# Sliding-window attention on one core: two key blocks folded into one score tile, parted again on GpSimd

## The chip, the core and the metric

The kernel runs on one core of one Trainium2 chip. A core has TensorE (PE, matrix products into PSUM), VectorE (DVE), ScalarE (ACT), GpSimd (POOL, no access to PSUM) and SyncE (SP, which issues the transfers here). Each engine works through its own list of instructions in a fixed order and waits on semaphores for the others. The metric is the device time of one execution in microseconds.

## The reference

Two decoder layers over 1024 tokens of width 1024. Each layer has a token-mixing part, of which one half is attention with eight query heads of 64, two key/value heads and a learned sink per head; the other half is a pooling mixer; then an output projection and a SwiGLU feed-forward. The attention is what the change touches:

```python
diff = qi + BLOCK - kj                      # qi: query in its block of 128, kj: key in two blocks of 128
valid = (diff >= 0) & (diff < WINDOW) & (key_abs >= 0)          # WINDOW = 128
scores = jnp.where(valid, q @ k_cat * HEAD_DIM ** -0.5, NEG_INF)
probs = softmax(concatenate([scores, sink], -1))[..., :-1]
out = probs @ v_cat
```

A query of index i in its block sees, of its own block, the keys 0 to i, and, of the block before, the keys i+1 to 127. So of the 256 keys of the two blocks exactly 128 are seen, one for every key index: own block's where the index is at most i, the other block's where it is larger. In block 0 there is no block before.

## The kernel before, in words

All products are made in split precision: an operand is copied to a rounded high part (`hi`, on ScalarE) and a low part (`lo = x - hi`, on VectorE), by the helper `split` (L220, L221), and a product is three matmuls, hi x hi, hi x lo, lo x hi (`mm3`, L263, L266, L267). Tokens go in two halves of 512 (four blocks of 128 each).

`attention` is a generator that is advanced in step with the dense products (`run` in the layer loop), so that its small matmuls stand among the large ones. Half 0 runs beside the projections of the pooling input and of half 1's queries and keys; half 1 starts beside the output projection of half 0 and goes on beside the projections and the first feed-forward products that follow. It works through groups: a group is one block and one key/value head, four query heads. For a group it

- splits and transposes the queries (`att_queries`, L842 to L851), and at a new block rotates (`att_rotary`, L795 to L800, through a tile `rt`) and transposes the keys of both heads (`att_keys`); the values lie padded with zeros in `vz`, filled by GpSimd casts (L808);
- makes the scores of two heads at a time (`att_scores`): per head two matmuls of 256 columns, both blocks side by side (L866, L867), and one VectorE instruction that adds the mask, scales and takes the row maximum (L869);
- a group later, takes the softmax (`att_softmax`): the sink enters the maximum and the sum by small VectorE steps (L881 to L890) and an exponential (L885); four exponentials of 256 columns on ScalarE (L888), three scalings on VectorE (L894) and one on ScalarE (L896);
- transposes the probabilities of two heads, four tiles of 128x128 (`att_probs`, L904), and splits them into `pth` and `ph` (512 columns: two blocks, two heads);
- multiplies by the values (`att_values`): per block and pair of heads three matmuls of 256 columns, all into one bank `pv`.

In block 0 only the own block's half of all this is done.

What sets the order is the framework's scheduler: it takes the instructions in program order as their priority, plays the program through by its own table of costs, and writes one fixed list for each engine; extra orders within an engine are set by `after`. A tile's tag has a fixed number of buffers (`SMALL`, `SHARED`, `REGIONS`), and a new tile waits until the last use of the one whose buffer it takes.

## Time and profile before

| what | value |
|---|---|
| median of three runs | 1906.67 us (1903.42, 1906.67, 1907.11) |
| span of the profiled execution | 1904.4 us |
| TensorE, VectorE, ScalarE, GpSimd busy | 1864.7, 1540.4, 948.4, 20.0 us |
| mean granted TensorE clock | 0.994 |
| attention, layer 0 | about 66 to 296 us |
| attention, layer 1 | about 1000 to 1236 us |

The page gives the span of one profiled execution (1904.4 us), and no other time of that execution; it lies within the three runs, 2.3 us under their median. Rows of groups read: line, engine, operation, output <- inputs, shapes, count | busy time, mean ns of one | idle time before them and what ended it. Rows of the timeline read: start, duration, engine, line, operation, and in brackets idle time before it. Matmuls are pipelined, so that the durations of neighbours overlap; on the other engines, too, an instruction's listed end lies a little behind the next one's start.

### The profile page before, as it was taken

The numbers are of one execution on the slowest core, as the hardware profiler recorded it, in microseconds if no ns is written. First come the engines' busy times: TensorE is split into PE (matmuls) and PEld (weight loads), VectorE is DVE, ScalarE is ACT, GpSimd is POOL, SyncE is SP. The second block draws the span as 40 slices with busy tenths as digits, with TensorE's granted clock in tenths as the row PEclk, the third lists the DMA queues.
The fourth block names the chain that finished last, engine by engine and source line by source line (L and its number), as shares of the span: only waits on it lengthen the run. The fifth ranks groups of instructions, "written<-read, shape, count | busy, mean of one in ns | idle before, by whom it ended". The sixth has DMA issues, their size and how long they took to land.

```text
span 1904.4 us, 26019 instructions
## 1 busy us (share of the span) xinstructions
PE 1864.7 (98%) x8954; PEld 1540.3 (81%) x8954; DVE 1540.4 (81%) x2889; ACT 948.4 (50%) x1791; POOL 20.0 (1%) x67
## 2 busy tenths in 40 slices
PE   7999999999999999999999999999999999999998
PEld 5887788888888788888888868888887888888886
DVE  7899886668898888788879988846888888867687
ACT  4875795654222223445558667845622222234452
POOL 0000000000000000000000000000000000000000
PEclk9999999999999999999999989999999999999999
DMA  9345563655555665944554464536654565574343
GB/s 341 112 144 161 161 221 125 191 172 193 194 183 188 205 210 172 320 143 150 172 179 139 126 181 164 178 111 209 214 189 146 198 216 197 199 249 157 117 141 114
DMA packets 229540, 341.86 MB, mean 180 GB/s; under 512 B 17016, under 2 KB 126472, under 8 KB 229408
## 3 DMA queue, kind: packets, MB, share of 16 engines
q1 hardware_dynamic: 228800, 338.10, 53.8%
q10 hardware_dynamic: 576, 2.10, 0.3%
q8 instruction: 70, 1.15, 0.3%
q14 instruction: 62, 0.51, 0.1%
q0 software_dynamic: 32, 0.00, 0.0%
HBM read 267.25 MB, written 72.89 MB: 179 GB/s over the span
## 4 chain that ended last, share of the span: by engine, by line
PE 80%; DVE 10%; DMA 5%; ACT 3%; issue 2%; SPq 0%; DVEq 0%; ACTq 0%; POOL 0%; POOLq 0%
PE acc L263 25%; PE acc L266 24%; PE acc L267 24%; DMA ar<-in_ada_w_dram 2%; DVE lo L221 1%; DVE ada L298 1%; DMA raw<-in_w_up_dram 1%; PE msc L904 1%; PE msc L561 1%; ACT hi L220 1%; PE pv L263 1%; PE pv L266 1%; PE pv L267 1%; ACT raw L554 1%; DVE fn L1162 1%
## 5 line engine op out<-in xcount | busy, mean ns | idle before, releaser
L220 ACT ACTIVATE hi<-raw 128x1024 fp32r<-128x1024 f32 (+1 forms) x388 | 331.8, 868 | 360.1 <-PE acc L266 197.1
L221 DVE TENSOR_TENSOR lo<-raw,hi 128x1024 fp32r<-128x1024 f32 (+1 forms) x388 | 380.2, 987 | 121.3 <-ACT hi L220 116.4
L263 PE MATMUL acc<-t,hi 128*128 128x512 f32 x704 | 274.6, 390 | 2.7 <-ACT hi L220 2.6
L266 PE MATMUL acc<-t,hi 128*128 128x512 f32 x704 | 274.0, 389 | 0.0
L267 PE MATMUL acc<-t,lo 128*128 128x512 f32 x704 | 271.8, 389 | 0.0
L263 PE MATMUL acc<-bh,hi 128*128 128x512 f32 x520 | 202.8, 390 | 0.0
L267 PE MATMUL acc<-bh,lo 128*128 128x512 f32 x520 | 202.4, 389 | 0.0
L263 PE MATMUL acc<-hT,hi 128*128 128x512 f32 x480 | 190.2, 396 | 0.6 <-DVE fn L691 0.6
L266 PE MATMUL acc<-hT,hi 128*128 128x512 f32 x480 | 188.4, 392 | 0.0
L267 PE MATMUL acc<-hT,lo 128*128 128x512 f32 x480 | 187.6, 392 | 0.0
L1162 DVE TENSOR_TENSOR fn<-acc,fn 128x512 f32<-128x512 f32 x220 | 150.3, 685 | 38.2 <-PE acc L267 37.6
L263 PEld LDWEIGHTS acc<-t,hi 128*128 128x128 f32 x704 | 132.2, 188 | 32.1 <-ACT hi L220 5.1
L267 PEld LDWEIGHTS acc<-t,lo 128*128 128x128 f32 x704 | 132.2, 188 | 28.7 <-DVE lo L221 1.2
L266 PEld LDWEIGHTS acc<-t,hi 128*128 128x128 f32 x704 | 132.2, 188 | 27.1
L266 PE MATMUL acc<-ph,hi 128*128 128x512 f32 x320 | 124.7, 390 | 0.0
L1098 ACT ACTIVATE fn<-fn 128x512 f32<-128x512 f32 x44 | 27.9, 633 | 181.7 <-DVE fn L1162 181.7
L263 PEld LDWEIGHTS acc<-bh,hi 128*128 128x128 f32 x520 | 97.6, 188 | 20.2
L267 PEld LDWEIGHTS acc<-bh,lo 128*128 128x128 f32 x520 | 97.6, 188 | 20.2
L298 DVE SCALAR_TENSOR_TENSOR ada<-ar,c_act,ada 128x512 f32<-128x512 f32 x140 | 104.6, 747 | 10.1 <-DMA ar<-in_ada_w_dram 9.7
L263 PE MATMUL acc<-hi 128*128 128x512 f32 x256 | 103.5, 410 | 2.4 <-DVE fn L691 2.0
L263 PEld LDWEIGHTS acc<-hT,hi 128*128 128x128 f32 x480 | 90.2, 188 | 19.2 <-DVE fn L691 1.4
L267 PEld LDWEIGHTS acc<-hT,lo 128*128 128x128 f32 x480 | 90.1, 188 | 18.6 <-issue 0.2
(323 smaller groups left out, 3814.5 us busy)
## 6 DMA issues: line engine op xcount, KB each, us to landing
ar<-in_ada_w_dram SPq DMA_DIRECT2D x160, 256.0 KB
raw<-in_w_gate_dram SPq DMA_DIRECT2D x44, 512.0 KB
raw<-in_w_up_dram SPq DMA_DIRECT2D x44, 512.0 KB
raw<-in_w_in_dram SPq DMA_DIRECT2D x80, 256.0 KB
raw<-keeps SPq DMA_DIRECT2D x40, 512.0 KB
keeps<-fn SPq DMA_DIRECT2D x66, 256.0 KB
two_b<-in_w_down_dram SPq DMA_DIRECT2D x30, 512.0 KB
raw<-keepa SPq DMA_DIRECT2D x25, 512.0 KB
```

The lines of the kernel that those rows point to most:

```text
L220: a = nc.scalar.activation(hi, src, AF.Copy)
L221: v = nc.vector.tensor_sub(lo, src, hi.bitcast(F32))
L263: ins = nc.tensor.matmul(dst, lh, rh, start=first, stop=False)
L266: nc.tensor.matmul(dst, lh, rl, start=False, stop=False)
L267: return nc.tensor.matmul(dst, ll, rh, start=False, stop=last)
L298: ins = nc.vector.scalar_tensor_tensor(acc, w, c_act[:, i : i + 1], acc, op0=ALU.mult, op1=ALU.add)
L554: nc.scalar.activation(hf, bank, AF.Identity, bias=shift, scale=scale)
L561: ins = nc.tensor.transpose(bank[:, t * P : (t + 1) * P], src[t], ident)
L904: nc.tensor.transpose(bank[:, i * P : (i + 1) * P], s[:, ii, ck * P : (ck + 1) * P], ident)
L1098: nc.scalar.activation(g, g, AF.Silu)
L1162: nc.vector.tensor_add(halves_of(dst)[m], bank, halves_of(src)[m])
```

## The change

For a group the scores of both blocks are still made, 256 columns a head. Then they are folded into one tile `S` of 128 columns a head: ScalarE copies the scores of the block before out of PSUM (L865 of the changed kernel; in block 0 a GpSimd fill with -1e30 instead), and VectorE copies the own block's scores over them where the 0/1 mask `own` is set (L869, a predicated copy). The sink stands in column 128 of each head, put there by a GpSimd copy and divided by the scale beforehand, so the maximum (L873, one instruction for four heads), the exponentials (L881, 129 columns) and the sums take it along. One VectorE instruction scales the 4x128 probabilities (L885). They are transposed as four tiles of 128x128 (L893) and split once, both parts in `pth`. GpSimd parts them: L906 writes the own block's part (zero elsewhere) of the high and the low half into two new tiles, L911 then zeroes that part in place, which leaves the block before. In block 0 only the own part is kept, in place (L899). The value products are six matmuls of 512 columns, the own block first.

The small tiles change too: `rt` goes, and the rotation uses the unused end of the `S` tile; `pth` has four buffers for two, `st` nine for twelve; the 128x256 mask becomes a 128x128 one.

```diff
-    SMALL = dict(junk=1, st=12, rs=8, ...)
+    SMALL = dict(junk=1, st=9, rs=8, ...)
-        mix=dict(..., vz=5, rt=1, qT=1, pth=2, pwh=1, pwl=1),
+        mix=dict(..., vz=5, qT=1, pth=4, pwh=1, pwl=1),
...
+    own = const.tile([P, P], F32, name="own")
+    nc.gpsimd.memset(own, 1.0)
     nc.gpsimd.affine_select(
+        out=own, in_=own, pattern=[[-1, P]], compare_op=ALU.is_ge,
+        fill=0.0, base=0, channel_multiplier=1,
     )
...
-    def att_scores(blk, n, u, qT, mx, s):
+    def att_scores(blk, u, qT, kT, S):
...
-        for ii in range(2):
-            nc.vector.tensor_tensor_reduce(
-                out=s[:, ii, cs], in0=bank[:, ii * 2 * P : (ii + 1) * 2 * P][:, cs],
-                in1=mask[:, cs], scale=SCALE, scalar=-3.0e38, op0=ALU.add, op1=ALU.max,
-                accum_out=mx[:, 2 * u + ii : 2 * u + ii + 1],
-            )
+        both = bank.rearrange("p (i o k) -> p i o k", i=2, o=2)
+        dst = S[:, 2 * u : 2 * u + 2, 0:P]
+        if blk:
+            nc.scalar.activation(dst, both[:, :, 0, :], AF.Copy)
+        else:
+            nc.gpsimd.memset(dst, NEG)
+        seen = own.bitcast(I32).rearrange("p (o k) -> p o k", o=1).to_broadcast([P, 2, P])
+        nc.vector.copy_predicated(dst, seen, both[:, :, 1, :])
+
+    def att_max(S):
+        mx = t_("st", [P, 8])[:, :GRP]
+        nc.vector.tensor_reduce(mx, S, axis=mybir.AxisListType.X, op=ALU.max)
+        nc.vector.tensor_scalar(mx, mx, -SCALE, None, op0=ALU.mult)
+        return mx
+
+    def att_softmax(S, nm):
+        sm = t_("st", [P, 8])[:, :GRP]
+        es = t_("st", [P, 8])[:, :GRP]
+        for i in range(GRP):
+            nc.scalar.activation(
+                S[:, i, :], S[:, i, :], AF.Exp, bias=nm[:, i : i + 1], scale=SCALE, accum_out=sm[:, i : i + 1]
             )
...
+        nc.vector.reciprocal(es, sm)
+        nc.vector.tensor_mul(
+            S[:, :, 0:P], S[:, :, 0:P], es.rearrange("p (i o) -> p i o", o=1).to_broadcast([P, GRP, P])
         )
...
+        for i in range(GRP):
+            nc.tensor.transpose(bank[:, i * P : (i + 1) * P], S[:, i, 0:P], ident)
+        seen = [t_("pth", [P, 512], F32R) for _ in range(2)]
+        split(*seen, bank)
+        views = [r.rearrange("p (i q) -> p i q", i=GRP) for r in seen]
...
+        here = [t_("pth", [P, 512], F32R) for _ in range(2)]
+        for v, r in zip(views, here):
+            nc.gpsimd.affine_select(
+                out=r.rearrange("p (i q) -> p i q", i=GRP), in_=v, pattern=[[0, GRP], [1, P]],
+                compare_op=ALU.is_ge, fill=0.0, base=0, channel_multiplier=-1,
+            )
+        for v in views:
+            nc.gpsimd.affine_select(
+                out=v, in_=v, pattern=[[0, GRP], [-1, P]], compare_op=ALU.is_gt,
+                fill=0.0, base=0, channel_multiplier=1,
+            )
+        return [seen, here]
...
-        for ck in range(first, 2):
+        for ck in (1, 0) if blk else (1,):
...
             ins = mm3(
-                pv[:, u * 2 * P : (u + 1) * 2 * P],
-                vh[:, vs].rearrange("p a d -> p (a d)"), vl[:, vs].rearrange("p a d -> p (a d)"),
-                ph[:, cs], pl[:, cs], opening, closing, None if opening else attn["open"],
+                pv, vh[:, vs].rearrange("p a d -> p (a d)"), vl[:, vs].rearrange("p a d -> p (a d)"),
+                *probs[ck], opening, closing, None if opening else attn["open"],
             )
...
-    def attention(h, qkvs, nsink, cat):
+    def attention(h, qkvs, sink, cat):
...
+                both = t_("sb", [P, D])
+                S = both[:, : GRP * (P + 1)].rearrange("p (i k) -> p i k", i=GRP)
+                room = both[:, GRP * (P + 1) :]
...
+                nc.gpsimd.tensor_copy(S[:, :, P : P + 1], sink[:, hs].rearrange("p (i o) -> p i o", o=1))
                 yield
+            flush()
             if prev:
-                att_softmax(pblk, pn, sts, mx, nsink)
+                att_softmax(prev[3], prev[4])
                 yield
...
-                flush()
-                if prev:
-                    late.append((pblk, pn, u, att_probs(pblk, sts[u]), cat, pt))
+                if prev and u == 0:
+                    late.append((prev[0], prev[1], att_probs(prev[0], prev[3]), cat, prev[2]))
```

Since the scheduler places every instruction anew, the order shows what the diff does not. TensorE, layer 0, half 1, the last but one group, before: the transposes of the second pair of heads (L904) stand between the first value products of the first pair.

```order
L904 MATMUL msc<-ident,sb 128x128 x2
L263 MATMUL pv<-pth,vz 128x256
L904 MATMUL msc<-ident,sb 128x128 x2
L263 MATMUL acc<-hT,hi 128x512
L266 MATMUL acc<-hT,hi 128x512
L267 MATMUL acc<-hT,lo 128x512
L266 MATMUL pv<-ph,vz 128x256
L267 MATMUL pv<-pth,vz 128x256
L263 MATMUL pv<-pth,vz 128x256
```

Here three dense matmuls lie between the products with the high part and those with the low part. The same group on TensorE in the changed kernel (lines are five to eleven lower; L893 are the transposes, L860 and L861 the next group's scores, L258, L261 and L262 the three matmuls of `mm3`):

```order
L893 MATMUL msc<-ident,sb 128x128 x4
L860 MATMUL msc<-sa,qT 128x256
L861 MATMUL msc<-sa,qT 128x256
L860 MATMUL msc<-sa,qT 128x256
L861 MATMUL msc<-sa,qT 128x256
L261 MATMUL acc<-hT,hi 128x512
L262 MATMUL acc<-hT,lo 128x512
L258 MATMUL acc<-hT,hi 128x512
L261 MATMUL acc<-hT,hi 128x512
L262 MATMUL acc<-hT,lo 128x512
L258 MATMUL pv<-pth,vz 128x512
L258 MATMUL acc<-hT,hi 128x512
```

All four transposes come together, then four score matmuls and five dense ones, then the first value product; three dense matmuls separate it from the other five, which follow each other. GpSimd at about the same place, before:

```order
L808 CAST vz<-vz_zero 128x64 x6
L784 COPY uT<-halo 128x16
L808 CAST vz<-vz_zero 128x64 x4
L784 COPY uT<-halo 128x16 x3
L808 CAST vz<-vz_zero 128x64 x5
```

and in the changed kernel:

```order
L965 COPY sb<-sk 128x4
L906 AFFINE_SELECT pth<-pth 128x512 x2
L911 AFFINE_SELECT pth<-pth 128x512 x2
L803 CAST vz<-vz_zero 128x64 x2
L965 COPY sb<-sk 128x4
L906 AFFINE_SELECT pth<-pth 128x512 x2
L911 AFFINE_SELECT pth<-pth 128x512 x2
```

Between the casts that it had, GpSimd now has four selections for each group, the own block's high and low part first, and the sink's copy for a group to come ahead of them.

More of the change, by code (lines that the diff above doesn't have):

```diff
@@ L96, in hybrid_decoder_kernel @@
     dr = ctx.enter_context(tc.tile_pool(name="dr", bufs=1, space=DRAM))
-    SMALL = dict(junk=1, st=12, rs=8, ss=4, halo=8, rows=1, cols=2, colp=4, sk=2)
+    SMALL = dict(junk=1, st=9, rs=8, ss=4, halo=8, rows=1, cols=2, colp=4, sk=2)
     SHARED = dict(hT=8, fn=4, raw=2, hi=3, lo=3, sa=2, sb=2, ar=2, ada=1, ph=3, G=1)
     REGIONS = dict(
-        mix=dict(cfa=2, cfb=2, qkv=5, bqkv=1, uT=4, pt=2, vz=5, rt=1, qT=1, pth=2, pwh=1, pwl=1),
+        mix=dict(cfa=2, cfb=2, qkv=5, bqkv=1, uT=4, pt=2, vz=5, qT=1, pth=4, pwh=1, pwl=1),
         up=dict(t2=8, t1=8, t3=8, b22=8, t4=8),
@@ L157, in hybrid_decoder_kernel @@
     ones = ones_r.bitcast(F32)
-    pick_row = t_("rt", [P, 7])
+    pick_row = t_("pth", [P, 7])
     nc.vector.memset(pick_row, 0.0)
@@ new lines, in att_scores @@
+            nc.tensor.matmul(dst, q, kT[1][:, cs], start=False, stop=True)
+        both = bank.rearrange("p (i o k) -> p i o k", i=2, o=2)
[11 more added lines that the diff above has]
+        return mx
@@ L898, in att_probs @@
-    def att_probs(blk, s):
-        bank = msc_bank()
-        for ck in range(0 if blk else 1, 2):
-            for ii in range(2):
-                i = 2 * ck + ii
-                nc.tensor.transpose(
-                    bank[:, i * P : (i + 1) * P], s[:, ii, ck * P : (ck + 1) * P], ident
-                )
-        ph = t_("pth", [P, 512], F32R)
-        pl = t_("ph", [P, 512], F32R)
-        cs = slice(0 if blk else 2 * P, 4 * P)
-        split(ph[:, cs], pl[:, cs], bank[:, cs])
-        return ph, pl
@@ L913, in att_values @@
-    def att_values(blk, n, u, probs, cat, t):
-        if n == 0 and u == 0:
+            nc.tensor.transpose(bank[:, i * P : (i + 1) * P], S[:, i, 0:P], ident)
+        seen = [t_("pth", [P, 512], F32R) for _ in range(2)]
+        split(*seen, bank)
+        views = [r.rearrange("p (i q) -> p i q", i=GRP) for r in seen]
+        if not blk:
+            for v in views:
+                nc.gpsimd.affine_select(
+                    out=v, in_=v, pattern=[[0, GRP], [1, P]], compare_op=ALU.is_ge,
+                    fill=0.0, base=0, channel_multiplier=-1,
+                )
+            return [None, seen]
@@ L1477, in hybrid_decoder_kernel @@
         qkvs[1] = [t_("qkv", [P, QKV]) for _ in range(NT)]
-        att = attention(0, qkvs[0], par["nsink"], cats[0][0])
+        att = attention(0, qkvs[0], par["sink"], cats[0][0])
         def dense():
@@ L1494, in hybrid_decoder_kernel @@
         fn, ss, out0 = mix_out(l, cats[0], G)
-        att = attention(1, qkvs[1], par["nsink"], cats[1][0])
+        att = attention(1, qkvs[1], par["sink"], cats[1][0])
         run(out0, 2 * KD, (side, 4 * ADA), (att, 16))
```

70 lines of the change are left out of this document (23 added, 47 removed).

## The prediction

> **What bounds the kernel now.** I read the page's busy shares first, then a table of stretches around the attention, then single groups and stretches of the timeline.
>
> ```profile
> PE 1864.7 (98%) x8954; PEld 1540.3 (81%) x8954; DVE 1540.4 (81%) x2889; ACT 948.4 (50%) x1791; POOL 20.0 (1%) x67
> core 0: us, PE busy (x) PEld busy (x) DVE busy (x) ACT busy (x) POOL busy (x), PEclk, DMA share, GB/s
> 66.00:158.00 92.00, 90.36 (x572) 77.88 (x571) 85.86 (x259) 72.12 (x181) 3.33 (x11) 1.00 0.43 130
> 158.00:200.00 42.00, 37.38 (x172) 28.30 (x171) 38.23 (x99) 25.54 (x60) 0.00 (x0) 0.92 0.60 176
> 200.00:296.00 96.00, 94.37 (x529) 78.78 (x529) 81.32 (x226) 80.29 (x191) 2.99 (x9) 1.00 0.58 191
> 296.00:940.00 644.00, 642.39 (x2862) 530.08 (x2861) 520.25 (x726) 262.26 (x394) 0.00 (x0) 1.00 0.57 190
> 1098.00:1140.00 42.00, 38.09 (x167) 29.15 (x168) 38.81 (x100) 26.95 (x65) 0.70 (x1) 0.88 0.64 185
> 1140.00:1236.00 96.00, 94.45 (x529) 79.09 (x528) 76.93 (x212) 77.38 (x181) 2.73 (x8) 1.00 0.52 174
> ```
>
> TensorE carries the kernel: 98% busy, and 642.39 of 644 us in the long feed-forward stretch, which the change does not touch. The attention lies in 66 to 296 us and, for layer 1, up to 1236 us. There TensorE is still busy 98% of the time, but VectorE is at 85.86 of 92 us and ScalarE at 80.29 of 96: three engines are near their limit together, and GpSimd is idle. In 158 to 200 and 1098 to 1140 the granted clock falls to 0.92 and 0.88.
>
> Busy TensorE time cannot be used as a price, since matmuls overlap. The price is the step from one start to the next:
>
> ```profile
> L904 PE MATMUL msc<-ident,sb 128*128 128x128 f32 x240 | 41.1, 276 | 2.6 <-DVE sb L894 2.1 <-ACT raw L554 0.6
> L263 PE MATMUL pv<-pth,vz 128*128 128x256 f32 x120 | 35.9, 299 | 1.9 <-ACT pth L220 1.8
> 109.14 0.40 PE L263 MATMUL acc<-hi,hT 128*128 128x512 f32 x1
> 109.37 0.40 PE L266 MATMUL acc<-lo,hT 128*128 128x512 f32 x1
> 143.89 0.28 PE L263 MATMUL pv<-pth,vz 128*128 128x256 f32 x1
> 144.01 0.28 PE L266 MATMUL pv<-ph,vz 128*128 128x256 f32 x1
> 144.61 0.60 PE L904 MATMUL msc<-ident,sb 128*128 128x128 f32 x4
> 144.97 0.36 PE L263 MATMUL acc<-hi,hT 128*128 128x256 f32 x1
> ```
>
> A 512-column matmul steps 0.23 us (109.14 to 109.37), a 256-column one 0.12 us, and four transposes of a 128x128 tile 0.36 us (144.61 to 144.97), so 0.09 us each, although each is listed with some 0.28 us.
>
> **The change, part by part.** A group is four heads of one 128-query block. There are 32 in two layers: 28 in blocks that see a block before them, 4 in block 0.
>
> TensorE. Transposes fall from 240 to 128: 112 x 0.09 = 10.1 us less. The value products become half as many, twice as wide: twelve of 256 columns (12 x 0.12 = 1.44 us) against six of 512 (6 x 0.23 = 1.38 us), and in block 0 six against three; with 30 times that it is some 2.2 us by the finer steps (0.120 and 0.227). Scores stay. Sum: **-12.3 us**. By the mean durations it would be 112 x 0.276 + 180 x 0.2 = 67 us, which is the trap in this profile.
>
> VectorE and ScalarE, also by steps:
>
> ```profile
> L869 DVE CUSTOM_DVE_ANT_0 sb<-msc,mask 128x256 f32<-128x256 f32 x112 | 44.2, 416 | 7.8 <-PE msc L867 7.4
> L888 ACT ACTIVATE sb<-sb,st 128x256 f32<-128x256 f32 x112 | 55.6, 502 | 5.9 <-DVE st L881 5.9
> L888 ACT ACTIVATE sb<-sb,st 128x128 f32<-128x128 f32 x16 | 6.2, 390 | 0.0
> 139.93 0.17 DVE L890 RECIPROCAL st<-st 128x4 f32<-128x4 f32 x1
> 140.01 0.39 DVE L869 CUSTOM_DVE_ANT_0 sb<-msc,mask 128x256 f32<-128x256 f32 x1
> 140.33 0.87 DVE L894 TENSOR_SCALAR sb<-sb,st 128x256 f32<-128x256 f32 x3
> 141.12 0.69 DVE L1002 TENSOR_TENSOR pt<-pt 128x521 f32<-128x521 f32 x1
> 141.74 0.68 DVE L763 TENSOR_TENSOR qkv<-acc,bqkv 128x512 f32<-128x512 f32 x1
> 142.35 0.69 DVE L221 TENSOR_TENSOR ph<-msc,pth 128x512 fp32r<-128x512 f32 x1
> 246.10 0.40 ACT L842 ACTIVATE hi<-qkv 128x256 fp32r<-128x256 f32 x1
> 246.89 0.51 ACT L896 ACTIVATE sb<-sb,st 128x256 f32<-128x256 f32 x1 [0.38 <-DVE st L890]
> ```
>
> VectorE loses per group four masked maxima (4 x 0.32, 140.01 to 140.33), one of two splits (0.61, 141.74 to 142.35), three scalings (0.79, 140.33 to 141.12) and two small steps (2 x 0.08): 2.84 us. It gains two predicated copies, one maximum over 4x129 and one scaling of 4x128. None stands in the trace. A predicated copy has the size and source of the masked maximum, so 0.32 us; above, 0.61 us if it went at the step of a 512-column operation. The other two read 512 columns like the rows of 0.61. That is 1.86 us, or 2.44 us at the upper end: **0.4 to 1.0 us less a group**, 11 to 28 us less in 28 groups. ScalarE loses 0.11 us on each exponential (502 against 390 ns), the sink's own exponential, the scaling (about 0.4 us, like L842's 0.40) and one split (0.60 us, at 141.72 below), and gains two copies of 256 columns (0.40 each at most): some 0.7 us less a group, about 20 us in all. Both engines have slack against TensorE over a whole stage, and the score-to-transpose chain gets a copy, a separate maximum and a negation (0.40 + 0.61 + 0.08) while losing as much (0.44 in exponentials, 0.4 in the scaling, the sink's small steps). I take **0** for the path, with -4 us as the other end, for the stage at 200 us where ScalarE is fullest.
>
> GpSimd takes over the masking: four selections of 128x512 a group, two in block 0, so 120, plus 32 sink copies and 8 fills.
>
> ```profile
> masks.py:199 POOL TENSOR_SCALAR_AFFINE_SELECT G<-G 128x128 f32<-128x128 f32 x1 | 0.3, 299 | 0.1
> L166 POOL TENSOR_SCALAR_AFFINE_SELECT mask<-mask 128x256 f32<-128x256 f32 x1 | 0.4, 391 | 0.0
> 2.97 0.41 POOL L808 CAST vz<-vz_zero 128x64 fp32r<-128x64 f32 x2
> 955.25 2.24 POOL L808 CAST vz<-vz_zero 128x64 fp32r<-128x64 f32 x4 [680.14 <-ACT hT L220]
> 955.24 0.69 DVE L221 TENSOR_TENSOR hT<-ada,hT 128x512 fp32r<-128x512 f32 x1 [1.51 <-ACT hT L220]
> 955.85 1.37 DVE L221 TENSOR_TENSOR lo<-raw,hi 128x512 fp32r<-128x512 f32 x2
> 141.19 0.49 PE L904 MATMUL msc<-ident,sb 128*128 128x128 f32 x3
> 141.72 0.60 ACT L220 ACTIVATE pth<-msc 128x512 fp32r<-128x512 f32 x1 [1.03 <-PE msc L904]
> ```
>
> A selection of 128 columns takes 299 ns, of 256 columns 391 ns: 0.72 ns a column, so **0.58 us** for 512. But GpSimd is slower beside a busy VectorE: two casts alone take 0.41 us, four beside three VectorE operations with two SBUF inputs take 2.24 us, so three of them waited about (2.24 - 4 x 0.2) / 3 = 0.48 us each. A selection then costs 0.58 us alone and about **1.06 us** when its turn falls behind such an operation.
>
> The other way round, VectorE's two splits took 1.37 us for an expected 0.61 + 0.69 = 1.30: about 0.04 us lost to each 64-column cast. A selection has eight times the columns: by that 0.3 us, at the lower end 0.04, at the upper the whole 0.58. With six in ten of VectorE's operations in these stages reading two SBUF tensors (an estimate from the splits from raw, the ada sums and the pool sums among the groups), 120 x 0.3 x 0.6 = 22 us go back to VectorE, about what the folding saved. VectorE as a whole stands where it was. The Trainium skill ("SBUF — State Buffer", "Who interferes with whom") says that a VectorE operation with two SBUF inputs and a GpSimd operation that reads SBUF lock each other out for the whole instruction; the casts agree for GpSimd, and no run here has yet shown the whole instruction for VectorE.
>
> **Where a new wait falls.** The four selections stand between the split and the value products, which are queued on TensorE in a fixed order with dense matmuls behind them. From the last transpose's start (141.19 plus two steps, 141.4) ScalarE's split ends 0.9 us later (142.32) and VectorE's 1.6 us later (142.35 + 0.69). Selection 1 needs the first, 2 the second; 3 and 4 follow in the queue. The fifth product needs selection 4. Without contention that is 1.6 + 3 x 0.58 = 3.3 us after the transposes; with each of three selections behind a VectorE operation, 1.6 + 3 x 1.06 = 4.8 us. In the order shown ahead of this prediction, for the last but one group of a half, TensorE does 4 x 0.12 + 5 x 0.23 before the first product and seven 512-column steps more before the fifth: 3.2 us. So TensorE waits 0.1 to 1.6 us there; I take 0.8. The last two groups of each half are like that: eight groups, 6.4 us. About eight others have 2.7 to 3.5 us of matmuls ahead of the first product; at the contended end they wait 4.8 - 4.0 = 0.8, at the other nothing: 0.25, 2 us. The rest have 6 us or more and do not wait. What TensorE waited for the old split (1.9 us on L263 pv) goes. **+6.5 us**, between -2 (no new wait) and 8 x 1.6 + 8 x 0.8 - 1.9 = +17.
>
> **Sum.** 1904.4 - 12.3 + 0 + 6.5 = 1898.6 against the profiled span. The span is 2.3 us under the median of the runs shown, so I forecast **1901 us**, 0.3% faster.
>
> **Rivals.**
> (1) *The dense stages do not let TensorE's saving through.* VectorE at 93% in 66 to 158 us, and the low clock with the ada sums in 158 to 200, set those stages. Against it: TensorE is at 98% in the same stage. The second halves of the two layers hold 16 of the 28 groups, some six of them in the slow stretches; if only the other ten pass the saving on, it is 10/28 x 12.3 = 4.4 us, the waits take 4 back, and the time is 1906: no change.
> (2) *GpSimd and VectorE block each other.* If every selection holds VectorE for its whole 0.58 us, 120 x 0.58 x 0.6 = 42 us go onto VectorE against 11 to 28 saved; in stages with 93% busy I count half of the 14 to 31 us excess on the path, 11 us, and the products wait at their contended end, 17 us: 1904.4 - 12.3 + 11 + 17 + 2.3 = **1922**; with half of each added cost, 1908, still no change. It decides from the point at which a selection takes over about 0.9 us in its stage. For it: the four casts. Against it: the 0.04 us.
> (3) *The waits vanish.* The planner put other matmuls between the products; -12.3 - 2 - 4 gives 1888.
>
> **How the numbers follow.** Forecast and its near neighbours (1893 to 1903) 0.44, rival 3 0.09, rival 1 0.21, rival 2 0.26. No change means within 0.2% (3.8 us), about what runs of this kernel can tell. The forecast and rival 3 are faster, 0.52 without the forecast's upper edge of 0.01; rival 1 and that edge make 0.22; slower is 0.26. The range leaves one in ten on either side: from 1886, under rival 3, to 1916, more than halfway to the end of rival 2. The likeliest case's own range is 1893 to 1903.
>
> **What would show it.** Right: selections of 0.6 to 1.1 us in the listing; 128 transposes at a step of 0.09; TensorE's idle time before the value products released by POOL, 5 to 10 us over both layers; VectorE's busy time lower by at most 30 us. Wrong: selections of over 1.2 us or VectorE rows of the splits longer than 0.75 us on the mean (rival 2); stages at 66 and 1000 us not shorter (rival 1); no wait released by POOL at all (rival 3). A predicated copy of over 0.7 us would also break the sum.

## The result: slightly slower, where slightly faster was forecast

| | before | changed |
|---|---|---|
| median of 20 runs each | 1907.76 us (1903.42 to 1911.28) | 1911.7 us (1909.27 to 1918.39) |
| ratio to before, 95% interval | 1 | 1.0024 (1.0017 to 1.0031) |
| span of the profiled execution | 1904.4 us | 1911.0 us |

Forecast were 1901 us and 0.3% faster, with 26 in 100 for slower. The profiled execution of the kernel before was a quick one: a run's time lies 1.7 to 2.2 us above its span in the runs here, so its span of 1904.4 us answers to some 1906 us, while the medians of its runs beside the changed kernel and the experiments were 1907.8 to 1909.7 us. So every kernel is compared by its ratio to the runs of the kernel before on the same chip, and traces only stretch by stretch.

The page of the changed kernel gives the busy times, and a table of stretches around the attention the same by stage (columns as before the change):

```profile
PE 1853.3 (97%) x8662; PEld 1516.5 (79%) x8662; DVE 1533.0 (80%) x2569; ACT 923.5 (48%) x1755; POOL 125.7 (7%) x226
```

```profile
66.00:158.00 92.00, 87.87 (x497) 71.23 (x495) 85.27 (x189) 65.61 (x173) 26.57 (x46) 1.00 0.42 130
158.00:200.00 42.00, 37.34 (x176) 29.39 (x177) 37.30 (x82) 25.61 (x68) 4.82 (x9) 0.92 0.61 175
200.00:296.00 96.00, 90.50 (x448) 72.43 (x447) 77.85 (x159) 71.63 (x174) 26.72 (x42) 0.98 0.56 183
1000.00:1098.00 98.00, 93.47 (x540) 77.02 (x538) 90.44 (x196) 67.74 (x177) 28.94 (x52) 1.00 0.44 132
```

TensorE has 292 matmuls less and is busy 11.4 us less, and yet the span is longer: TensorE now stands idle where it worked. ScalarE is 25 us lighter (948.4 to 923.5; forecast: about 20). VectorE, which lost four masked maxima, three scalings and a split per group, is only 7.4 us lighter, and in the stretch at 66 us it still works 85.27 of 92 us (before: 85.86).

The groups of the changed kernel that the steps of the prediction spoke of:

```profile
L893 PE MATMUL msc<-ident,sb 128*128 128x128 f32 x128 | 19.5, 275 | 3.1 <-DVE sb L885 1.5 <-DVE pt L1019 0.8 <-ACT hi L215 0.7
L258 PE MATMUL pv<-pth,vz 128*128 128x512 f32 x60 | 26.1, 436 | 1.5 <-POOL pth L911 1.4
L261 PE MATMUL pv<-pth,vz 128*128 128x512 f32 x60 | 25.7, 428 | 4.1 <-POOL pth L911 3.3 <-POOL pth L906 0.5
L911 POOL TENSOR_SCALAR_AFFINE_SELECT pth<-pth 128x512 fp32r<-128x512 f32 x56 | 46.1, 846 | 0.0
L906 POOL TENSOR_SCALAR_AFFINE_SELECT pth<-pth 128x512 fp32r<-128x512 f32 x56 | 41.0, 732 | 49.6 <-ACT pth L215 45.0 <-DVE pth L216 3.3
L899 POOL TENSOR_SCALAR_AFFINE_SELECT pth<-pth 128x512 fp32r<-128x512 f32 x8 | 6.7, 858 | 4.4 <-DVE pth L216 4.4
L869 DVE COPY_PREDICATED sb<-own,msc 128x256 f32<-128x256 int32 x64 | 28.4, 444 | 6.3 <-ACT sb L865 6.0 <-issue 0.2
L873 DVE TENSOR_REDUCE st<-sb 128x4 f32<-128x516 f32 x32 | 21.8, 681 | 0.2
L885 DVE TENSOR_TENSOR sb<-sb,st 128x512 f32<-128x512 f32 x32 | 21.9, 685 | 0.3
```

The prices that the prediction had to bound came out close to it: a selection 0.73 to 0.86 us on the mean, a predicated copy like the masked maximum it replaces (444 ns, from 416), the reduction and the scaling like any 512-column operation. TensorE's idle time before the value products that GpSimd released is 1.4 + 3.3 + 0.5 = 5.2 us. The forecast had 8.4 us of it (6.4 + 2), and took off the 1.9 us of the old wait to get 6.5; by the rows the net is 5.2 - 1.9 = 3.3 us.

**Which stretch lost it.** The dense matmuls (into `acc`) are the same 7368 in every kernel here. Counting them off and comparing when the same one starts gives what each stretch of the program gained or lost against the profiled execution of the kernel before. The stretches are named by their times there; "rest" is all outside the attention, some 3 to 7 us in almost every kernel, of which the quick profiled execution of the kernel before explains some 2 to 4.

| us against before | 66-165 | 165-210 | 210-310 | 990-1110 | 1110-1150 | 1150-1250 | attention | rest |
|---|---|---|---|---|---|---|---|---|
| changed kernel | +2.2 | -4.0 | +3.6 | +2.5 | -3.7 | +1.3 | +1.9 | +4.7 |
| no selections | -3.4 | -3.9 | -1.1 | +0.4 | -3.7 | -2.6 | -14.3 | +4.4 |
| selections unread | +0.6 | -2.3 | +0.5 | +1.8 | -3.3 | +0.3 | -2.4 | +5.2 |
| no selections, 25 us of VectorE work added | +0.0 | -1.1 | +0.7 | +2.5 | -4.3 | +1.1 | -1.1 | +6.8 |
| no selections, transposes back | -0.5 | -3.9 | +3.0 | -1.1 | -3.4 | +4.5 | -1.4 | +12.5 |
| difference of the values | -2.6 | -4.0 | -0.1 | +0.2 | -5.8 | -0.2 | -12.5 | +3.6 |

The changed kernel is slower in the four stretches where selections run beside the dense products, and quicker in the two between the halves. The gain between the halves does not come from the saved transposes, since it is there with the transposes back as well (-3.9 and -3.4). The other rows are experiments, told next.

### The profile page after: what moved, and what is told of

Same layout as the page of the kernel before. It is cut to its first block, busy times and chain, and to the rows that moved or that the text cites. A ratio compares the mean times of both kernels' runs of the same rounds, so it can differ in the third digit from the quotient of the medians.

```text
span 1911.0 us, 25332 instructions
## 1 busy us (share of the span) xinstructions
PE 1853.3 (97%) x8662; PEld 1516.5 (79%) x8662; DVE 1533.0 (80%) x2569; ACT 923.5 (48%) x1755; POOL 125.7 (7%) x226
## 4 chain that ended last, share of the span: by engine, by line
PE 72%; DVE 14%; DMA 5%; ACT 3%; issue 2%; POOL 1%; SPq 1%; POOLq 0%; DVEq 0%; ACTq 0%
PE acc L258 23%; PE acc L261 23%; PE acc L262 22%; DVE lo L216 2%; DMA raw<-in_w_up_dram 2%; DVE ada L293 2%; DMA ar<-in_ada_w_dram 2%; PE msc L556 1%; ACT hi L215 1%; DVE fn L1169 1%; DMA raw<-in_w_in_dram 1%; POOL pth L911 1%; DVE pth L216 1%; PE pv L261 0%; ACT sb L881 0%
## 5 line engine op out<-in xcount | busy, mean ns | idle before, releaser
L215 ACT ACTIVATE hi<-raw 128x1024 fp32r<-128x1024 f32 (+1 forms) x388 | 332.1, 868 | 371.5 <-PE acc L261 194.4
L216 DVE TENSOR_TENSOR lo<-raw,hi 128x1024 fp32r<-128x1024 f32 (+1 forms) x388 | 383.0, 994 | 123.4 <-ACT hi L215 120.2
L258 PE MATMUL acc<-t,hi 128*128 128x512 f32 x704 | 274.6, 390 | 4.8 <-ACT hi L215 4.8
L261 PE MATMUL acc<-t,hi 128*128 128x512 f32 x704 | 274.0, 389 | 0.0
L262 PE MATMUL acc<-t,lo 128*128 128x512 f32 x704 | 272.0, 390 | 0.0
L258 PE MATMUL acc<-bh,hi 128*128 128x512 f32 x520 | 202.8, 390 | 0.0
L262 PE MATMUL acc<-bh,lo 128*128 128x512 f32 x520 | 202.4, 389 | 0.0
L258 PE MATMUL acc<-hT,hi 128*128 128x512 f32 x480 | 190.5, 397 | 1.2 <-DVE fn L686 1.2
L261 PE MATMUL acc<-hT,hi 128*128 128x512 f32 x480 | 188.5, 393 | 0.0
L262 PE MATMUL acc<-hT,lo 128*128 128x512 f32 x480 | 188.2, 392 | 0.0
L258 PEld LDWEIGHTS acc<-t,hi 128*128 128x128 f32 x704 | 132.1, 188 | 34.2 <-ACT hi L215 7.2
L262 PEld LDWEIGHTS acc<-t,lo 128*128 128x128 f32 x704 | 132.1, 188 | 29.3 <-DVE lo L216 1.9
L261 PEld LDWEIGHTS acc<-t,hi 128*128 128x128 f32 x704 | 132.1, 188 | 27.2
L261 PE MATMUL acc<-ph,hi 128*128 128x512 f32 x320 | 124.7, 390 | 0.0
L293 DVE SCALAR_TENSOR_TENSOR ada<-ar,c_act,ada 128x512 f32<-128x512 f32 x140 | 108.7, 777 | 6.7 <-DMA ar<-in_ada_w_dram 5.7
L262 PEld LDWEIGHTS acc<-bh,lo 128*128 128x128 f32 x520 | 97.6, 188 | 20.5
L258 PEld LDWEIGHTS acc<-bh,hi 128*128 128x128 f32 x520 | 97.6, 188 | 20.1
L258 PEld LDWEIGHTS acc<-hT,hi 128*128 128x128 f32 x480 | 90.6, 189 | 20.2 <-DVE fn L686 2.5
L262 PEld LDWEIGHTS acc<-hT,lo 128*128 128x128 f32 x480 | 90.5, 189 | 18.6
L261 PEld LDWEIGHTS acc<-hT,hi 128*128 128x128 f32 x480 | 90.7, 189 | 17.3
```

Of the source, the lines that this page charges most:

```text
L215: a = nc.scalar.activation(hi, src, AF.Copy)
L216: v = nc.vector.tensor_sub(lo, src, hi.bitcast(F32))
L258: ins = nc.tensor.matmul(dst, lh, rh, start=first, stop=False)
L261: nc.tensor.matmul(dst, lh, rl, start=False, stop=False)
L262: return nc.tensor.matmul(dst, ll, rh, start=False, stop=last)
L293: ins = nc.vector.scalar_tensor_tensor(acc, w, c_act[:, i : i + 1], acc, op0=ALU.mult, op1=ALU.add)
```

## The experiments

Each time is a median, and each ratio is to runs of the kernel before on the same chip.

**Without selections.** First the whole price of GpSimd's part: `att_probs` returns the unparted probabilities, which are then multiplied by both blocks' values (the masking of the values is left out).

```diff
         split(*seen, bank)
-        views = [r.rearrange("p (i q) -> p i q", i=GRP) for r in seen]
-        if not blk:
...
-        here = [t_("pth", [P, 512], F32R) for _ in range(2)]
-        for v, r in zip(views, here):
-            nc.gpsimd.affine_select(
...
-        return [seen, here]
+        return [seen, seen]
```

> The changed kernel without any of the 120 selections: the value products read the unparted probabilities for both blocks, so the masking of the values is left out. Theory 'selections' (waiting or blocking): all that GpSimd costs goes, 9 to 13 us less, 1899 to 1903 us, and TensorE's saving of 12 us shows in full against the kernel before. Theory 'tail': the chain of the last group loses its 2 x 2.2 us of selections but keeps the table loads, 1906 to 1909 us. If the dense stages do not let TensorE's saving through (rival 1 of the prediction): 1905 to 1908 us.

Measured: 1896.24 us, ratio 0.9934 (0.9916 to 0.9951), 12.6 us faster than before. The page of this kernel:

```profile
PE 1846.8 (97%) x8662; PEld 1515.0 (80%) x8662; DVE 1511.5 (80%) x2569; ACT 925.6 (49%) x1755; POOL 32.1 (2%) x106
```

Selections and all that hangs on them cost 0.90% of 1909 us, 17 us. VectorE has the same 2569 instructions as in the changed kernel and is busy 1511.5 us instead of 1533.0: the selections lengthen it by 21.5 us. With GpSimd out of the way the folding comes through. What of it is TensorE's and what VectorE's, this run does not tell.

**Selections that nobody reads.** They have two prices: products that wait for them, and VectorE held up beside them. Here all 120 run, but into tiles that no product reads (masking again left out).

```diff
-        for v in views:
+        for v, r in zip(views, here):
             nc.gpsimd.affine_select(
-                out=v, in_=v, pattern=[[0, GRP], [-1, P]], compare_op=ALU.is_gt,
+                out=r.rearrange("p (i q) -> p i q", i=GRP), in_=v, pattern=[[0, GRP], [-1, P]], compare_op=ALU.is_gt,
...
-        return [seen, here]
+        return [seen, seen]
```

> The changed kernel with as many selections on GpSimd, written to two tiles that no product reads: the value products read the unparted probabilities, so the masking of the values is left out, but GpSimd works as before beside VectorE. If the cost of the selections is that the products wait for them: as without selections, within 2 us (1899 to 1904 us). If it is that GpSimd and VectorE block each other: close to the changed kernel, 1908 to 1912 us.

Measured: 1909.26 us, ratio 0.9997 (0.9987 to 1.0007). So of the 17 us, 0.63% or 12 us stay although nothing waits for a selection; what is left for the waiting is the other 0.27%, 5 us. By stretches of the traces it is 11.9 and 4.3. The page, and the value products, which now wait for GpSimd nowhere:

```profile
PE 1851.3 (97%) x8662; PEld 1516.2 (79%) x8662; DVE 1531.5 (80%) x2569; ACT 926.5 (49%) x1755; POOL 127.6 (7%) x226
```

```profile
L258 PE MATMUL pv<-pth,vz 128*128 128x512 f32 x60 | 25.2, 420 | 1.8 <-ACT pth L215 1.7
L261 PE MATMUL pv<-pth,vz 128*128 128x512 f32 x60 | 24.0, 399 | 0.0
```

The unread copies take as many `pth` buffers as the changed kernel's, but a lack of buffers is not what costs: of the 19.8 us that ScalarE stood idle before its splits into `pth` (L215), the transposes ended 19.3, and of VectorE's 4.7 us before its part (L216), ScalarE's split 4.3.

How VectorE is held can be seen in single instructions of the changed kernel. Two places on its timeline, GpSimd first, then VectorE (start, duration, and idle time before in brackets):

```profile
94.28 1.22 POOL L899 TENSOR_SCALAR_AFFINE_SELECT pth<-pth 128x512 fp32r<-128x512 f32 x2 [1.17 <-DVE pth L216]
206.41 1.42 POOL L906 TENSOR_SCALAR_AFFINE_SELECT pth<-pth 128x512 fp32r<-128x512 f32 x2 [0.54 <-ACT pth L215]
207.78 1.67 POOL L911 TENSOR_SCALAR_AFFINE_SELECT pth<-pth 128x512 fp32r<-128x512 f32 x2
94.46 0.46 DVE L869 COPY_PREDICATED sb<-own,msc 128x256 f32<-128x256 int32 x1 [0.25 <-ACT sb L865]
94.95 0.69 DVE L873 TENSOR_REDUCE st<-sb 128x4 f32<-128x516 f32 x1
207.25 1.12 DVE L293 SCALAR_TENSOR_TENSOR ada<-ar,c_act,ada 128x512 f32<-128x512 f32 x1
209.29 0.75 DVE L293 SCALAR_TENSOR_TENSOR ada<-ar,c_act,ada 128x512 f32<-128x512 f32 x1 [0.92 <-DMA ar<-in_ada_w_dram]
```

At 94 us VectorE works on two operations that read one SBUF tile each (the copy reads the mask there and its data from PSUM): two selections take 1.22 us, 0.61 each, and VectorE's rows keep their 0.46 and 0.69. At 207 us an ada sum, two SBUF inputs, takes 1.12 us instead of the 0.75 of the same line two microseconds later, and the two selections beside it 1.67 us instead of 1.22, so that one of them takes 1.06 if the other keeps its 0.61. Both sides lose some 0.4 us. The means over the kernel say the same. Three groups of VectorE, each first without selections and then with the unread ones: the split that reads two SBUF tiles, the maximum that reads one, and the small negation of the maximum (four columns):

```profile
L216 DVE TENSOR_TENSOR hT<-raw,hT 128x512 fp32r<-128x512 f32 x32 | 21.5, 687 | 12.8 <-ACT hT L215 12.8
L216 DVE TENSOR_TENSOR hT<-raw,hT 128x512 fp32r<-128x512 f32 x32 | 23.8, 759 | 12.1 <-ACT hT L215 11.8
L873 DVE TENSOR_REDUCE st<-sb 128x4 f32<-128x516 f32 x32 | 22.0, 686 | 0.3
L873 DVE TENSOR_REDUCE st<-sb 128x4 f32<-128x516 f32 x32 | 21.9, 683 | 0.3
L874 DVE TENSOR_SCALAR st<-st 128x4 f32<-128x4 f32 x32 | 5.3, 164 | 0.1
L874 DVE TENSOR_SCALAR st<-st 128x4 f32<-128x4 f32 x32 | 7.4, 231 | 0.1
```

The Trainium skill ("SBUF — State Buffer", "Who interferes with whom") has a VectorE operation with two SBUF inputs and a GpSimd operation that reads SBUF contend for a lock, and one with a single SBUF input run free of it unless it is in a mode that uses two ports. The split, the ada sum and the maximum agree. The negation has one SBUF input and got longer all the same; whether by such a mode is not shown.

**Twice as many.** The same kernel with every unread selection done twice (240 in all; block 0's eight are doubled with them).

```diff
+        for v, r in zip(views, here):
+            nc.gpsimd.affine_select(
+                out=r.rearrange("p (i q) -> p i q", i=GRP), in_=v, pattern=[[0, GRP], [1, P]],
...
+        for v, r in zip(views, here):
+            nc.gpsimd.affine_select(
+                out=r.rearrange("p (i q) -> p i q", i=GRP), in_=v, pattern=[[0, GRP], [-1, P]], compare_op=ALU.is_gt,
...
         return [seen, seen]
```

> The kernel with unread selections, each done twice: 240 instead of 120, and no product waits for any (the masking of the values is left out). If a selection costs about 0.1 us on the path by what it takes from VectorE (13 us for 120): 13 us more than with 120, 1920 to 1924 us. If the first 120 only took what was already lost (the cost levels off): 1909 to 1913 us. VectorE's busy time grows by another 20 us in both.

Measured: 1936.03 us, ratio 1.0145 (1.0130 to 1.0159): 28 us more, twice the linear forecast, not less. The page:

```profile
PE 1858.4 (96%) x8662; PEld 1522.7 (79%) x8662; DVE 1564.7 (81%) x2569; ACT 925.8 (48%) x1755; POOL 228.3 (12%) x346
```

VectorE grew by 33.2 us for the second 120, after 20.0 for the first, and most of that comes through: the price rises with the load. Where TensorE pays can be read before its own small matmuls, the transposes of the queries (L841) and of the probabilities (L893), without selections, with the unread ones, and with twice as many:

```profile
L841 PE MATMUL msc<-ident,hi 128*128 128x128 f32 x128 | 16.2, 250 | 2.7 <-DVE hi L838 1.8 <-ACT hi L837 0.5 <-DVE sb L869 0.3
L893 PE MATMUL msc<-ident,sb 128*128 128x128 f32 x128 | 19.9, 276 | 2.7 <-DVE sb L885 1.6 <-ACT hi L215 0.7 <-DVE pt L1001 0.2
L841 PE MATMUL msc<-ident,hi 128*128 128x128 f32 x128 | 16.2, 250 | 5.3 <-DVE hi L838 4.5 <-ACT hi L837 0.5 <-DVE sb L869 0.3
L893 PE MATMUL msc<-ident,sb 128*128 128x128 f32 x128 | 19.8, 277 | 4.3 <-DVE sb L885 2.1 <-ACT hi L215 0.8 <-DVE pt L1020 0.7
L841 PE MATMUL msc<-ident,hi 128*128 128x128 f32 x128 | 16.2, 251 | 7.1 <-DVE hi L838 6.3 <-ACT hi L837 0.5 <-DVE sb L869 0.3
L893 PE MATMUL msc<-ident,sb 128*128 128x128 f32 x128 | 20.7, 286 | 12.9 <-DVE sb L885 9.7 <-DVE pt L1030 2.3 <-ACT hi L215 0.7
```

Over the whole attention, TensorE's idle time that VectorE ended is 11.5, 21.0 and 41.2 us in these three kernels.

**The same load, but planned.** Is it the holding, which the fixed order could not reckon with, or simply VectorE's time? Here there are no selections (masking left out), and the scaling of the probabilities is done a second time into a tile that nobody reads.

```diff
+        again = t_("pth", [P, 512], F32R)
+        nc.vector.tensor_mul(
+            again.rearrange("p (i k) -> p i k", i=GRP), S[:, :, 0:P],
+            es.rearrange("p (i o) -> p i o", o=1).to_broadcast([P, GRP, P]),
+        )
```

> The kernel without selections (the masking of the values left out), with the scaling of the probabilities done a second time on VectorE into a tile that nobody reads: 32 x 0.68 = 21.8 us of ordinary VectorE work, about the 21.5 us by which the selections lengthen VectorE's busy time (1533.0 against 1511.5 us). The planner knows of this work. Theory 'load' (a us on VectorE has its price on the path, whatever makes it): 10 to 13 us more than without selections, 1906 to 1909 us. Theory 'blocking' (only the holds that the fixed order did not reckon with cost): at most 3 us more, 1896 to 1899 us.

Measured: 1902.0 us, ratio 0.9965 (0.9953 to 0.9978), 5.9 us above the kernel without selections: between the two theories. The page:

```profile
PE 1846.9 (97%) x8662; PEld 1515.4 (80%) x8662; DVE 1528.7 (80%) x2601; ACT 922.1 (49%) x1755; POOL 33.5 (2%) x106
```

**Whose saving was it?** If VectorE's time has a price, then the 12.6 us without selections are not TensorE's alone. Two kernels part them, both without selections (masking left out). The first gives TensorE its work back, while VectorE keeps its relief: the transposes of a group are made twice.

```diff
-        for i in range(GRP):
+        for i in [*range(GRP)] * (2 if blk else 1):
             nc.tensor.transpose(bank[:, i * P : (i + 1) * P], S[:, i, 0:P], ident)
```

> The kernel without selections (the masking of the values left out), with the four transposes of a group made twice in the blocks that see a block before: 240 transposes as in the kernel before, 112 x 0.09 = 10.1 us of TensorE's work given back, while VectorE keeps its relief of 29 us. If TensorE's saving passes to the end in full: 9 to 11 us more than without selections, 1905 to 1908 us. If the gain of that kernel came from VectorE's relief: 1896 to 1900 us. Half and half: about 1901 to 1904 us.

Measured: 1911.62 us, ratio 1.0013 (1.0000 to 1.0027). The page and the group:

```profile
PE 1857.7 (97%) x8774; PEld 1529.5 (80%) x8774; DVE 1512.3 (79%) x2569; ACT 922.8 (48%) x1755; POOL 31.4 (2%) x106
```

```profile
L893 PE MATMUL msc<-ident,sb 128*128 128x128 f32 x240 | 33.1, 280 | 6.4 <-DVE sb L885 5.0 <-ACT hi L215 0.7
```

The gain is gone. In the attention the extra transposes cost 12.9 us against the kernel without selections (the table of stretches), for 10.1 us of TensorE time. The second set of transposes also stands between the scaling and the split of each group, so part of the 12.9 us may be the longer chain and not TensorE's time; the two are not told apart. Another 8 us of this profiled execution lie outside the attention, where nothing was changed; 5.6 us are the distance of this one execution (1917.25 us) from the median of its kernel, and the rest is not explained.

The second gives VectorE its work back, by a third, half-sized scaling a group besides the second one:

```diff
+        nc.vector.tensor_mul(
+            again[:, : 2 * P].rearrange("p (i k) -> p i k", i=2), S[:, :2, 0:P],
+            es[:, :2].rearrange("p (i o) -> p i o", o=1).to_broadcast([P, 2, P]),
+        )
```

> The other half of the same question: without selections, and with so much planned work on VectorE (a second and half a third scaling a group, 35 us by the rows) that it is as busy as before the change, about 1540 us, while TensorE keeps its saving. If TensorE's saving passes to the end by itself: 1896 to 1900 us. If the price of VectorE goes on as with the first 17 us (0.34 us a us): 1905 to 1907 us. If VectorE becomes the bound: over 1909 us, the whole gain gone.

Measured: 1909.49 us, ratio 1.0007 (0.9997 to 1.0017). The page:

```profile
PE 1855.0 (97%) x8662; PEld 1517.9 (79%) x8662; DVE 1536.5 (80%) x2633; ACT 922.0 (48%) x1755; POOL 34.3 (2%) x106
```

With VectorE at 1536.5 us, near the 1540.4 of before, nothing is left of the gain, though TensorE has none of the saved matmuls back and GpSimd hardly works. So TensorE's saving does not pass to the end by itself. Nor does VectorE's: as far as two kernels can tell, neither saving is worth anything alone, and together they were worth 12.6 us. The two losses, 15 and 14 us by the ratios, are three times what a mere reordering moved here (5 us, below). In these stages TensorE and VectorE bound the work together.

**The same result from half the selections.** The own part p1 of the probabilities p needs masking, the other part does not have to be made: p1 x V(own) + (p - p1) x V(before) = p x V(before) + p1 x (V(own) - V(before)). The second form needs L906 only, and its first three products none. The difference of the values is made once a block in `att_keys`, from the values less the high and the low part of the block before.

```diff
+            d = room[:, 0 : NKV * HD].rearrange("p (n d) -> p n d", d=HD)
+            for src, v in zip((vsrc, d), attn["v", blk - 1]):
+                nc.vector.tensor_sub(d, src, v[:, 0:3:2, :].bitcast(F32))
...
+            nc.scalar.activation(dh[:, 0:3:2, :], d, AF.Copy)
+            nc.vector.tensor_sub(dl[:, 0:3:2, :], d, dh[:, 0:3:2, :].bitcast(F32))
+            attn["d", blk] = (dh, dl)
...
-        for v in views:
-            nc.gpsimd.affine_select(
-                out=v, in_=v, pattern=[[0, GRP], [-1, P]], compare_op=ALU.is_gt,
...
         return [seen, here]
...
-        for ck in (1, 0) if blk else (1,):
+        for ck in (0, 1) if blk else (1,):
-            vh, vl = attn["v", blk - 1 + ck]
+            vh, vl = attn["d", blk] if blk and ck else attn["v", blk - 1 + ck]
```

> The same result from half the selections: the unparted probabilities times the values of the block before (no selection needed), plus the own part (two selections) times the difference of the two blocks' values, which is made once a block by two subtractions and a split of 128 columns. Theory 'selections, waiting': the first three products wait for nothing on GpSimd, and the last three for two selections instead of four: 5 to 8 us less, 1904 to 1907 us. Theory 'selections, blocking': half of GpSimd's work goes, some 2 to 4 us less after the added steps, 1908 to 1910 us. Theory 'tail': 1909 to 1911 us.

Measured: 1901.9 us, ratio 0.9952 (0.9937 to 0.9967). Run again beside other kernels:

> The kernel with the difference of the values once more, to see whether its gain against the kernel before holds on another chip and beside other runs: 0.994 to 0.997 of it, 1897 to 1903 us. If the first result was a lucky order or clock: 0.997 to 1.000.

Measured: 1897.09 us, ratio 0.9944 (0.9933 to 0.9956). This version beats both kernels, by 9 to 11 us the one before. The page of its first run, and the groups of the selections and of the first product that could wait for them:

```profile
PE 1845.8 (97%) x8662; PEld 1512.6 (80%) x8662; DVE 1526.9 (81%) x2611; ACT 927.7 (49%) x1769; POOL 93.1 (5%) x198
```

```profile
L917 POOL TENSOR_SCALAR_AFFINE_SELECT pth<-pth 128x512 fp32r<-128x512 f32 x56 | 42.9, 767 | 55.9 <-ACT pth L215 49.5 <-DVE pth L216 5.2
L261 PE MATMUL pv<-pth,vz 128*128 128x512 f32 x60 | 24.2, 404 | 0.2 <-POOL pth L917 0.2
```

The wait for GpSimd is 0.2 us instead of 5.2, and VectorE is at 1526.9 us in spite of 42 added small operations. It gained more than either expectation gave it, which fits its moving both prices at once; its ratio is about that of the kernel without selections that has the same VectorE load (1528.7 us, 0.9965).

**Two table loads in the tail.** The trace of the changed kernel had offered another culprit. Its scheduler put the first gated Silu of the feed-forward ahead of the last group's exponentials, so that ScalarE loads its tables twice more in each layer; before there was one such load at that place. ScalarE's row, and the last value products of layer 0 on TensorE (timeline):

```profile
L881 ACT ACT_TABLE_LOAD x4 | 5.1, 1283 | 2.0 <-issue 1.9
```

```profile
291.08 0.50 PE L261 MATMUL pv<-pth,vz 128*128 128x512 f32 x1 [0.16 <-POOL pth L906]
292.12 0.50 PE L258 MATMUL pv<-pth,vz 128*128 128x512 f32 x1 [0.31 <-POOL pth L911]
293.69 0.50 PE L261 MATMUL pv<-pth,vz 128*128 128x512 f32 x1 [0.84 <-POOL pth L911]
```

```diff
+        def gate():
+            g, u = halves_of(c)
+            nc.scalar.activation(g, g, AF.Silu) if "exp" not in recent else after(
+                nc.scalar.activation(g, g, AF.Silu), recent["exp"])
+            nc.vector.tensor_mul(g, g, u)
...
+            if put is not None:
+                gate()
...
-                g, u = halves_of(c)
-                gated(g, g, u)
+                put = p
```

> The changed kernel with one reordering: the first three gated Silus of the feed-forward are put behind the last exponential of the attention on ScalarE, so that the two extra table loads of 1.28 us in each layer go. TensorE's order stays. Theory 'tail' (the last group of the second half is late because its exponentials stand behind a Silu and two table loads): 4 x 1.28 = 5.1 us less, about 1906.6 us; the stretch before the last value product (294 and 1232 us) shrinks by some 2.6 us each. Theory 'selections' (TensorE waits for GpSimd's selections throughout): the products still wait for the selections, 1910 to 1912 us, no change.

Measured: 1914.09 us, ratio 1.0024 (1.0014 to 1.0034), exactly that of the changed kernel, with the four extra loads gone. The same edit on the kernel with the difference:

> The kernel with the difference of the values and the first gated Silus behind the last exponential, GpSimd's fills left where they were. If the four table loads are hidden, as in the first run of the study: within 2 us of the kernel beside it. If the tail sets the end here: 3 to 5 us less than it.

Measured: 1901.37 us, ratio 0.9968 (0.9957 to 0.9979), if anything slower than without it (0.9944 beside it). The tail theory has fallen: those loads stood in time that ScalarE had, and the last products waited 1.3 us in layer 0 for the selections, not for the tables. It also shows what a reordering with hardly any change of work does here: up to 0.24%, nearly 5 us. A difference of that size between two single kernels says little by itself.

**Filling on ScalarE.** GpSimd also fills the zero columns of the value tiles by casts of 128x64, 60 of them in the kernel with the difference. They were given to ScalarE.

```diff
-                nc.gpsimd.tensor_copy(v[:, 1, :], vz_zero)
+                nc.scalar.activation(v[:, 1, :], vz_zero, AF.Copy)
```

> The kernel with the difference of the values, with the 60 x 2 zero columns of the value tiles filled by ScalarE instead of GpSimd (GpSimd 21 us less busy, ScalarE some 20 us more). Theory 'blocking': GpSimd's casts hold VectorE too, 2 to 4 us less, 1898 to 1900 us. Theory 'ScalarE becomes late in the stage at 200 us': 1902 to 1906 us.

> As the kernel before in this set, and the first gated Silus behind the last exponential, so that two table loads of 1.28 us go in each layer. If the end of the attention sets the end of its stage once GpSimd is out of the way: 3 to 5 us less, 1894 to 1897 us. If the loads are hidden, as they were with four selections a group: no change, 1898 to 1901 us.

Measured: 1903.87 us, ratio 0.9982 (0.9972 to 0.9991), and with the Silus moved 1903.8 us, ratio 0.9976 (0.9966 to 0.9986). The first is 6 to 7 us worse by the ratios than the kernel it came from (0.9952 and 0.9944); the second is 1.5 us worse than its own partner with the Silus moved (0.9968), and there the intervals overlap. Neither is better, and the pages show VectorE no lighter (1528.5 and 1529.4 us, from 1526.9). Whether ScalarE's added work or the new order cost the first one its gain stays open.

## Why the prediction was wrong, step by step

The prices of single instructions were right, the sum was put together wrongly.

- **TensorE, -12.3 us.** The work did go: 112 transposes less, 11.4 us less busy. That the end would follow was argued from TensorE's 98%, and no run bears it out: with VectorE nearly as busy as before, the same saving was worth nothing (ratio 1.0007). Where VectorE was light, giving the transposes back cost at least their full time (12.9 us for 10.1).
- **VectorE and ScalarE, 0 for the path, because "both engines have slack against TensorE over a whole stage".** This is the step that failed. The folding itself took 1540.4 - 1511.5 = 28.9 us from VectorE (forecast: 11 to 28 in 28 groups), and 21.5 us came back through the holds (forecast: 22). The first lies at the upper end of its range, the second was met almost to the microsecond, and both were then given the price nothing. The runs put VectorE's busy time and the ratio side by side, with TensorE's matmuls the same in all five and no product waiting for GpSimd:

| VectorE busy, us | 1511.5 | 1528.7 | 1531.5 | 1536.5 | 1564.7 |
|---|---|---|---|---|---|
| kernel | no selections | planned load | unread selections | more planned load | unread, doubled |
| ratio to before | 0.9934 | 0.9965 | 0.9997 | 1.0007 | 1.0145 |

  That is a third of a microsecond on the path for each of the first 17, about one for one up to 1536.5, and over 0.9 beyond (0.0138 x 1909 / 28.2). The rise is shown; its shape is not, since single kernels move by up to 0.24% with their order. That held time is dearer than planned time is not shown either. The slack over the whole stage (85.86 of 92 us) was no slack: VectorE makes operands that TensorE's transposes and products need one by one, so a late operation there can become TensorE's idle time. Over the same dense products of the attention (66 to 310 and 990 to 1250 us of the kernel before), the traces give, in us:

| attention | before | no selections | unread selections | more planned load | changed |
|---|---|---|---|---|---|
| length | 503.7 | 489.4 | 501.2 | 502.7 | 505.6 |
| TensorE busy | 488.5 | 469.7 | 471.8 | 476.4 | 476.6 |
| TensorE idle | 15.2 | 19.7 | 29.5 | 26.3 | 28.9 |
| of it ended by VectorE | 8.5 | 11.5 | 21.0 | 14.6 | 13.7 |
| of it ended by ScalarE | 5.8 | 7.4 | 7.5 | 10.2 | 8.9 |
| of it ended by GpSimd | 0 | 0 | 0 | 0 | 5.3 |
| time at half clock | 17.1 | 10.2 | 10.2 | 17.1 | 17.1 |

  In the changed kernel TensorE works 11.9 us less here and stands idle 13.7 us more. Under held VectorE time most of the loss is idle time behind VectorE (21.0 from 11.5). Under planned load it is not: of 13.3 us, 6.6 are idle time, 3.1 of it behind VectorE and 2.8 behind ScalarE, and 6.7 are the same matmuls taking longer, of which 6.9 us more at half clock can explain 3.4. So the price of VectorE's load is shown there, and the way it reaches TensorE only in part. A busy share below 100% was taken for cover, on an engine that feeds the bound one operation by operation.
- **The new wait, +6.5 us.** The mechanism was right: TensorE stood idle before the value products until GpSimd was done, 5.2 us, within the 5 to 10 named as a sign. The size was half: 8.4 us had been reckoned before the old 1.9 us were taken off, and 5.2 - 1.9 is 3.3. What the wait costs the whole is less sure. The two timed kernels give 0.27%, 5 us, give or take 0.12%, and a mere reordering moved as much; and in the table above TensorE is idle no longer than with the unread selections (28.9 and 29.5 us), because less of the time is spent behind VectorE.
- **A selection, 0.58 us alone and 1.06 behind a VectorE operation with two SBUF inputs.** Right: 0.61 alone, 0.84 in the pair beside the ada sum, and means of 0.73 to 0.86 between those ends. The point from which rival 2 was to decide, over 0.9 us, was not reached, and neither was its 42 us on VectorE.
- **Rival 1** (the dense stages do not let TensorE's saving through, for VectorE at 93%) named the mechanism, and its mark came out: the stretches at 66 and 1000 us did not become shorter (+2.2 and +2.5 us). Its time, 1906, counted ten of 28 groups as free of it, those of the second halves outside the slow stretches; the stretches of these ten (from 210 and from 1150 us) were 3.6 and 1.3 us longer. Only between the halves, which it had counted among the slow ones, did the changed kernel gain time. So what happened is rival 1 in the four stretches beside the dense products, and the selections on top. By the ratios against 1908 us: -12.6 for the folding on all engines, +12.0 for VectorE held up and +5.1 for the wait, +4.5 us together, where 0.24% is 4.6. The 17 us of the selections are shown; how they part into 12 and 5 rests on the one kernel with unread selections.

The wait had been reckoned in. The other 12 us stood in the prediction too, as 22 us on VectorE, but were set off against what the folding saves there. That saving was not to spare: TensorE's own needed it to come through.

## What the runs showed of the hardware

TensorE's clock was granted at half speed for pieces of 3.4 us, now and then two in a row, each time behind a piece in which TensorE had been busy for only 0.8 to 2.2 us. Two neighbouring pieces between the halves, in the kernel before and then in the one with the difference (columns as above; the eighth is the clock):

```profile
162.00:165.40 3.40, 1.84 (x8) 1.04 (x9) 3.40 (x15) 3.00 (x7) 0.00 (x0) 1.00 0.57 154
165.40:168.80 3.40, 3.27 (x12) 2.33 (x11) 3.40 (x7) 3.03 (x6) 0.00 (x0) 0.50 0.56 154
```

```profile
162.50:165.90 3.40, 2.08 (x10) 1.16 (x10) 3.31 (x14) 3.40 (x8) 0.00 (x0) 1.00 0.50 149
165.90:169.30 3.40, 3.03 (x17) 2.52 (x17) 3.40 (x8) 1.79 (x4) 0.00 (x0) 1.00 0.51 131
```

VectorE is full there (3.40 and 3.31 of 3.40 us). In the first kernel TensorE waited 1.7 us for ScalarE's high part and 0.4 us for VectorE's low part of one operand, was busy for 1.84 us of the piece, and then ran at 0.50 through the next, which costs up to half of 3.4 us; in the second it was busy for 2.08 us and kept its clock. The Trainium skill ("TensorE: Matmul & The Clock Gate", "Part 1: The HAM clock gate") has the clock halved after an idle window of about 3.4 us; the length and the 0.50 agree, but the window here was not idle: TensorE was busy for 1.84 us of it. How much work in a piece keeps the clock is not shown: 2.16 us of it at 1127.9 us of the kernel before were followed by half clock, 1.88 us at 1203.1 us of the changed one were not. So a wait of TensorE can be paid for a second time, in clock. The traces' clock has five such pieces before the last matmuls in both the kernel before and the changed one, three without selections, six with the larger planned load and ten with the doubled selections: the seven more are up to 7 x 1.7 = 12 of the 40 us between the last and the one without selections.

## What to carry over

Where one engine makes operands for the bound one piece by piece, both bound the stage: price a saving by the later of the two, and find the price of a microsecond by adding idle work to one of them, before counting either as free. Work moved to GpSimd beside a busy VectorE is not free even if nobody waits for it: here 120 selections of 0.61 us alone lengthened VectorE by 20 us and the kernel by 12. Before masking on another engine, look for an algebra that needs less of it: multiplying the unparted probabilities and correcting by a difference nearly halved the selections and turned 0.24% slower into 0.5% faster.
